# Weight chunks fetched and summed two chunks ahead of their split, and the third weight sum kept in the tile of the activation sums

## The chip, the cores and the metric

The kernel runs on one core of a Trainium2 chip. The metric is the time of one execution on the device in microseconds (us), as the median of several runs.

## The reference, cut to what matters

The kernel computes a two-layer trunk over 512 positions with 1024 features, in float32. The first layer mixes with a spatial gate and pooling heads, the second with a short gated convolution. Every layer then attends into a memory of 256 positions and runs a gated feed-forward block, and each of the three sub-layers ends in a layer norm of `alpha * x + f(x)`. The change touches only the way in which weights are fetched, and the down projection of the feed-forward block:

```python
def conv_ffn(x, w_up, conv_w, conv_b, w_down):
    up = x @ w_up
    a, g = up[..., :D_FF], up[..., D_FF:]
    g = causal_dwconv(g, conv_w) + conv_b
    return (jax.nn.gelu(g) * a) @ w_down        # 512 x 2816 @ 2816 x 1024
...
x = layer_norm(alpha * x + conv_ffn(x, ...), ln_ffn_g[layer], ln_ffn_b[layer])
```

## The kernel before, in words

**Products.** Every operand of a matrix product is split into a high and a low part: ScalarE copies the float32 value to a rounded one (`split`, L80), and VectorE subtracts that from the value to get the rest (L81). One product of two operands is then three matmuls into the same PSUM tile (`mm3`, L194 to L196): high by high, high by low, low by high.

**Weights.** All weights pass through `Weights` in the order of a list, `plan`. A chunk is 128 partitions by 1024 columns, 512 KB. It is fetched by a DMA that SyncE's queue issues into a raw tile (pool `rpool`, seven buffers), and split into a pair of tiles `wh` and `wl` (pool `wpool`, `RING` = 5 buffers each). When a chunk has been used, `done()` calls `load()`, which issues the fetch, the sums if there are any, and the split of the chunk five places ahead. Across engines nothing but data and free tiles orders the work: SyncE issues a transfer as soon as its raw tile is free, so it runs ahead of the splits. Each engine works off its own queue in order. That order is laid out when the program is built, from the order of the code and from when each instruction is expected to be ready. A tile goes to its next user when the last reader of its last user is done, and tiles of one pool are handed out in the order of the code.

**The feed-forward block.** Its 22 hidden tiles go in three groups (`FFN_GROUPS`): two of eight, and one of six. For each group the up projection runs first (`ffn_up`; two chunks for each hidden tile, a gate and a value), then the group's part of the down projection. The groups of eight use seven block products in place of eight (`fast_product`), four times in the whole kernel: two groups in each of two layers. The third group is multiplied in the plain way.

**Sums of activations.** In `ffn_up` a `Blocks` object takes the hidden tiles of a group in four pairs. For each pair VectorE writes four blocks into one float32 tile named `blocks` (2048 columns, pool `fpool`, one buffer), makes four sums in it (L238) and splits seven of the eight blocks in one go (1792 columns), into tiles of the pool `apool`.

**Sums of weights.** For the same scheme GpSimd makes sums of weight blocks in `fast()`. The chunks of one product are, in the order of `fast_plan`: four `b11b21` with a first sum (t1, L148; one `t1t1` chunk for two of them); four `t2b22` with three sums each, where t3 = b22 - b12 (L153), t2 = t3 + b11 (L154, written over b12) and t4 = b21 - t2 (L155); one `t4t4` chunk behind each two of these; and two `t3t3` chunks. The sums t1, t3 and t4 of two chunks share a raw tile of their own. t3 is made with its `t2b22` chunk and used last.

**The product.** `fast_product` has three phases. Phase 1 takes the `b11b21` and `t1t1` chunks: 24 groups of three matmuls, into six PSUM tiles (X, Z, Y, two each). It ends in six adds to the rows `x` (L328, VectorE). Phase 2 takes `t2b22` and `t4t4`: for each `t2b22` chunk two groups with its first half (L365), two with its half of t4 (L367) and two with its second half (L369), 24 groups in all. X and Y go on in the same PSUM tiles, which the adds have read; Z gets new ones. Phase 3 takes `t3t3`, eight groups.

Of the kernel before, what the change touches and what calls it, by code (L numbers as in the profile page):

```python
# [8 lines left out]
F32 = mybir.dt.float32  # L9
# [5 lines left out]
P = 128  # L15
# [10 lines left out]
CH = 1024  # L26
ALPHA = 4.0**0.25
EPS = 1e-5
WINDOWS = (2, 4, 8, 16)
RING = 5  # L30
FFN_GROUPS = ((0, 8), (8, 16), (16, 22))
PAD = 16

# [2 lines left out]
def kernel(ctx: ExitStack, tc: tile.TileContext, a: dict, out: bass.AP):  # L36
    nc = tc.nc
# [4 lines left out]
    apool = ctx.enter_context(tc.tile_pool(name="apool", bufs=12))  # L42
    wpool = ctx.enter_context(tc.tile_pool(name="wpool", bufs=RING))
    rpool = ctx.enter_context(tc.tile_pool(name="rpool", bufs=7))
    gpool = ctx.enter_context(tc.tile_pool(name="gpool", bufs=1))
    tpool = ctx.enter_context(tc.tile_pool(name="tpool", bufs=4))
    fpool = ctx.enter_context(tc.tile_pool(name="fpool", bufs=1))
# [5 lines left out]
    def nm(s):  # L53
        uid[0] += 1
        return f"{s}{uid[0]}"
# [7 lines left out]
    def slot(dtype=F32R):  # L63

        return apool.tile([P, 2 * CH], dtype, tag="act", name=nm("act"))

    def duo(tag="act"):
        if tag == "act":
            t = slot()
            return t[:, :CH], t[:, CH:]  # L70
        h = wpool.tile([P, CH], F32R, tag="wh", name=nm("wh"))
        l = wpool.tile([P, CH], F32R, tag="wl", name=nm("wl"))
        return h, l

    def raw_tile():
        return rpool.tile([P, CH], F32, tag="raw", name=nm("raw"))

    def split(h, l, src):

        nc.scalar.copy(h, src)  # L80
        nc.vector.tensor_sub(l, src, h.bitcast(F32))  # L81

    def load_split(src, tag):
        raw = raw_tile()
        nc.sync.dma_start(raw, src)
        h, l = duo(tag)
        split(h, l, raw)
        return h, l
# [14 lines left out]
    plan = []  # L103
    for layer in range(2):
# [10 lines left out]
        plan += [("xa_wo", layer, n, i) for n in range(2) for i in range(4)]  # L115
        for m0, m1 in FFN_GROUPS:
            plan += [("ffn_w_up", layer, i) for i in range(2 * m0, 2 * m1)]
# [5 lines left out]
    class Weights:  # L123


        def __init__(self):
            self.ready, self.loaded, self.taken = [], 0, 0
            self.kept = {}

        def fast(self, what, layer, i):  # L130

            w = a["ffn_w_down"][layer]
            half = [slice(0, 512), slice(512, CH)]

            def fetch(src):
                t = raw_tile()
                nc.sync.dma_start(t[:, : src.shape[-1]], src)
                return t

            def both(key):  # L140

                if i % 2 == 0:
                    self.kept[key] = raw_tile()
                return self.kept[key][:, half[i % 2]]

            if what == "b11b21":
                w0, w1 = fetch(w[0, i]), fetch(w[1, i][:, half[0]])
                nc.gpsimd.tensor_sub(both("t1"), w1[:, half[0]], w0[:, half[0]])  # L148
                return w0
            if what == "t2b22":  # L150
                w1, w0, t3 = fetch(w[1, i]), fetch(w[0, i]), both(("t3", i // 2))
                b12 = t2 = w1[:, half[0]]
                nc.gpsimd.tensor_sub(t3, w1[:, half[1]], b12)  # L153
                nc.gpsimd.tensor_add(t2, t3, w0[:, half[0]])  # L154
                nc.gpsimd.tensor_sub(both("t4"), w0[:, half[1]], t2)  # L155
                return w1
            return self.kept.pop({"t1t1": "t1", "t4t4": "t4", "t3t3": ("t3", i // 2)}[what])

        def load(self, parts=1, other=None):

            if self.loaded == len(plan):
                return
            key = plan[self.loaded]
            self.loaded += 1
            if key[0] not in a:
                w = duo("w")
                split(*w, self.fast(*key))
                self.ready.append(w)
                return
            src = a[key[0]][key[1:]] if key[1:] else a[key[0]]  # L170
            both = ([other] if other else []) + [(src, duo("w"))]
            raws = [raw_tile() for _ in both]
            n = src.shape[-1] // parts
            for p in range(parts):
                c = slice(p * n, (p + 1) * n)
                for raw, (source, (h, l)) in zip(raws, both):
                    nc.sync.dma_start(raw[:, c], source[:, c])
                    split(h[:, c], l[:, c], raw[:, c])
            self.ready.append(both[-1][1])

# [9 lines left out]
    weights = Weights()  # L190
# [31 lines left out]
    class Blocks:  # L222
# [8 lines left out]

        def new(self):

            f = fpool.tile([P, 8, 256], F32, tag="blocks", name=nm("blocks"))

            def finish():
                def sub(to, x, y, op=ALU.subtract):
                    nc.vector.tensor_tensor(f[:, to, :], f[:, x, :], f[:, y, :], op=op)  # L238

                sub(self.S1, self.A21, self.A22, ALU.add)  # L240
                sub(self.S2, self.S1, self.A11)
                sub(self.S3, self.A11, self.A21)
                sub(self.S4, self.A12, self.S2)
                h, l = (slot()[:, : 7 * 256].rearrange("p (b s) -> p b s", b=7) for _ in range(2))
                self.pairs.append((h, l))
                split(h, l, f[:, :7, :])

            return [f[:, self.A11 :: self.A21, :], f[:, self.A12 : self.A22 + 1, :]], finish
# [303 lines left out]
    def load_mem():  # L552
        return [load_split(a["memT"][i], "act") for i in range(2)]
# [110 lines left out]
    def ffn_up(layer, xT, late, m0, m1):  # L664
        fast = m1 < NF
        hid = Blocks() if fast else Act(m1 - m0)
        m = m0
        while m < m1:
            n = 2 if m == 0 else 1
            ps = proj_batch([("ffn_w_up", layer, m * 2 + i) for i in range(2 * n)], xT, late if m == 0 else None)  # L670
            for i in range(n):
                g = tmp()
                conv3(g, ps[2 * i], lambda j: convw[:, layer, m, j : j + 1], convb[:, layer, m : m + 1])
                nc.scalar.activation(g, g, AF.Gelu_apprx_tanh)  # L674
                if fast:
                    if m % 2 == 0:
                        to, finish = hid.new()
                    halves = [v.rearrange("p (i s) -> p i s", i=2) for v in (g, ps[2 * i + 1])]
                    nc.vector.tensor_mul(to[m % 2], *halves)  # L679
                    if m % 2:  # L680
                        finish()
                else:
                    nc.vector.tensor_mul(g, g, ps[2 * i + 1])
                    split(hid.h(m - m0), hid.l(m - m0), g)
                m += 1
        return hid


    xT = Act(KD)
    for k in range(4):  # L690
        weights.load(2 if k < 2 else 1, (a["xT"][k], xT.tiles[k]))
    weights.done(RING - 4)

    late = None
    mem = []
    for layer in range(2):
        if layer == 0:
            y = mixer_ab(xT)
            xT, late = residual_norm([(lambda: y, 0, 8)], "ab_w_out", "ln_mix", layer, ahead=lambda: mem.append(load_mem()))
            kT = proj_k(layer, mem[layer], {2: late})  # L700
            late = None
        else:
            kT = proj_k(layer, mem[layer], {2: late})
            y = mixer_c(xT)
            xT, late = residual_norm([(lambda: y, 0, 8)], "c_w_out", "ln_mix", layer)
        o, hooks = attend(layer, xT, late, kT)
        xT, late = residual_norm([(lambda: o, 0, 8)], "xa_wo", "ln_xa", layer, hooks=hooks)
        up = [(lambda m0=m0, m1=m1, xT=xT, late=late: ffn_up(layer, xT, late, m0, m1), m0, m1) for m0, m1 in FFN_GROUPS]
        xT, late = residual_norm(up, "ffn_w_down", "ln_ffn", layer, layer == 1,
                                 ahead=None if layer else lambda: mem.append(load_mem()))  # L710
# [57 lines left out]
def build(shapes):  # L768
    import concourse.bacc as bacc

    nc = bacc.Bacc("TRN2", target_bir_lowering=False, num_devices=1)
    aps = {n: nc.dram_tensor(f"in_{n}", s, F32, kind="ExternalInput").ap() for n, s in shapes.items()}
    out = nc.dram_tensor("out_0_dram", (1, S, D), F32, kind="ExternalOutput").ap()
    with tile.TileContext(nc) as tc:
        kernel(tc, aps, out)
    return nc
# [9 lines left out]
```

## Time and profile before

| | |
|---|---|
| median of 3 runs | 1373.07 us (1372.56 to 1373.35) |
| the profiled execution's own time | 1371.29 us |
| its span, from the first to the last instruction | 1369.5 us |
| TensorE (matmul) busy | 1335.1 us, 97% of the span |
| VectorE busy | 842.1 us, 61% |
| ScalarE busy | 498.1 us, 36% |
| GpSimd busy | 153.5 us, 11% |
| granted TensorE clock, mean | 0.989 |

The profiled execution's time is some 1.8 us above its span, which counts only from the first to the last instruction. In the profile PE is TensorE's matmuls, PEld its weight loads, DVE is VectorE, ACT ScalarE, POOL GpSimd, and SP SyncE (SPq: its queue, which issues DMAs). L81 is line 81 of the kernel. Tile names stand without their numbers, so every raw tile is `raw`. A granted clock of 1.00 is 2.4 GHz and 0.50 is 1.2 GHz; between them lies a stretch that has some of each.

### The profile page before, as it was taken

The numbers are of one execution on the slowest core, as the hardware profiler recorded it, in microseconds if no ns is written. First come the engines' busy times: TensorE is split into PE (matmuls) and PEld (weight loads), VectorE is DVE, ScalarE is ACT, GpSimd is POOL, SyncE is SP. The second block draws the span as 40 slices with busy tenths as digits, with TensorE's granted clock in tenths as the row PEclk, the third lists the DMA queues.
The fourth block names the chain that finished last, engine by engine and source line by source line (L and its number), as shares of the span: only waits on it lengthen the run. The fifth ranks groups of instructions, "written<-read, shape, count | busy, mean of one in ns | idle before, by whom it ended". The sixth has DMA issues, their size and how long they took to land.

```text
span 1369.5 us, 16418 instructions
## 1 busy us (share of the span) xinstructions
PE 1335.1 (97%) x6526; PEld 1130.9 (83%) x6526; DVE 842.1 (61%) x1102; ACT 498.1 (36%) x671; POOL 153.5 (11%) x132
## 2 busy tenths in 40 slices
PE   8999999999989998999999999999999989998996
PEld 6888888898868886888988888988898868886885
DVE  6668456576576656556744447565776675576446
ACT  5343345244333333342522222354243433342330
POOL 1102000011240123000100001000101420141001
PEclk9999999999999999999999999999999999999999
DMA  9533433133344234433523331542142253326201
GB/s 361 157 123 114 164 126 108 59 109 98 102 150 142 85 95 159 139 108 93 200 93 97 103 93 48 168 139 78 47 154 93 93 186 106 95 88 202 94 0 62
DMA packets 47454, 161.88 MB, mean 118 GB/s; under 512 B 5648, under 2 KB 5776, under 8 KB 47376
## 3 DMA queue, kind: packets, MB, share of 16 engines
q1 hardware_dynamic: 45648, 154.53, 35.0%
q0 software_dynamic: 1728, 6.29, 1.4%
q8 instruction: 51, 0.84, 0.2%
q14 instruction: 27, 0.22, 0.1%
HBM read 158.70 MB, written 2.10 MB: 117 GB/s over the span
## 4 chain that ended last, share of the span: by engine, by line
PE 90%; POOL 4%; DMA 3%; DVE 2%; issue 1%; ACT 1%; POOLq 0%; DVEq 0%
PE ps L194 29%; PE ps L195 29%; PE ps L196 29%; DMA raw<-in_ffn_w_down 3%; POOL raw L154 1%; PE ps L313 1%; POOL raw L153 1%; DVE wl L81 1%; POOL raw L155 1%; ACT wh L80 1%; PE ps L633 1%; POOL rs L285 0%; DVE x L288 0%; PE ps L510 0%; DMA raw<-in_xT 0%
## 5 line engine op out<-in xcount | busy, mean ns | idle before, releaser
L81 DVE TENSOR_TENSOR wl<-raw,wh 128x1024 fp32r<-128x1024 f32 (+1 forms) x275 | 357.1, 1301 | 314.8 <-ACT wh L80 302.2
L80 ACT CAST wh<-raw 128x1024 fp32r<-128x1024 f32 (+1 forms) x275 | 287.4, 1045 | 561.7 <-PE ps L195 264.9
L194 PE MATMUL ps<-act,wh 128*128 128x512 f32 (+1 forms) x1316 | 478.8, 364 | 0.0
L195 PE MATMUL ps<-act,wh 128*128 128x512 f32 (+1 forms) x1316 | 478.4, 363 | 0.0
L196 PE MATMUL ps<-act,wl 128*128 128x512 f32 (+1 forms) x1316 | 478.3, 363 | 0.0
L194 PE MATMUL ps<-wh,act 128*128 128x512 f32 (+1 forms) x678 | 268.9, 397 | 23.9 <-DVE x L328 19.2
L194 PEld LDWEIGHTS ps<-act,wh 128*128 128x128 f32 x1316 | 248.5, 189 | 39.0
L196 PEld LDWEIGHTS ps<-act,wl 128*128 128x128 f32 x1316 | 248.5, 189 | 38.8
L195 PEld LDWEIGHTS ps<-act,wh 128*128 128x128 f32 x1316 | 248.5, 189 | 38.5
L195 PE MATMUL ps<-wl,act 128*128 128x512 f32 (+1 forms) x678 | 266.7, 393 | 0.0
L196 PE MATMUL ps<-wh,act 128*128 128x512 f32 (+1 forms) x678 | 266.4, 393 | 0.0
L194 PEld LDWEIGHTS ps<-wh,act 128*128 128x128 f32 x678 | 130.0, 192 | 52.5 <-DVE x L328 20.9
L196 PEld LDWEIGHTS ps<-wh,act 128*128 128x128 f32 x678 | 129.6, 191 | 27.0
L195 PEld LDWEIGHTS ps<-wl,act 128*128 128x128 f32 x678 | 129.9, 192 | 26.3 <-DVE wl L81 0.4
L285 POOL TENSOR_TENSOR rs<-rs,mhalf 128x1 f32<-128x1 f32 x28 | 39.9, 1428 | 824.6 <-DVE rs L284 824.6
L80 ACT CAST act<-ps 128x256 fp32r<-128x256 f32 (+1 forms) x144 | 62.9, 470 | 120.5 <-PE ps L313 79.2
L81 DVE TENSOR_TENSOR act<-ps,act 128x256 fp32r<-128x256 f32 (+1 forms) x144 | 73.0, 535 | 13.5 <-ACT act L80 13.1
L537 DVE SCALAR_TENSOR_TENSOR tmp<-ps,convw,tmp 128x511 f32<-128x511 f32 x88 | 65.6, 746 | 1.5
L674 ACT ACTIVATE tmp<-tmp 128x512 f32<-128x512 f32 x44 | 27.9, 633 | 96.9 <-DVE tmp L537 96.8
L148 POOL TENSOR_TENSOR raw<-raw,raw 128x512 f32<-128x512 f32 x16 | 27.0, 1688 | 269.4 <-DVE wl L81 216.2
L679 DVE TENSOR_TENSOR blocks<-tmp,ps 128x512 f32<-128x512 f32 x32 | 22.0, 687 | 46.3 <-PE ps L196 40.3
L81 DVE TENSOR_TENSOR act<-blocks,act 128x1792 fp32r<-128x1792 f32 x16 | 33.6, 2098 | 23.7 <-ACT act L80 23.7
(75 smaller groups left out, 763.2 us busy)
## 6 DMA issues: line engine op xcount, KB each, us to landing
raw<-in_ffn_w_up SPq DMA_DIRECT2D x88, 512.0 KB, 3.6
raw<-in_ffn_w_down SPq DMA_DIRECT2D x60, 512.0 KB, 3.6
raw<-in_c_w_in SPq DMA_DIRECT2D x24, 512.0 KB, 3.6
raw<-in_xa_wk SPq DMA_DIRECT2D x16, 512.0 KB, 3.7
raw<-in_xa_wq SPq DMA_DIRECT2D x16, 512.0 KB, 3.8
raw<-in_xa_wv SPq DMA_DIRECT2D x16, 512.0 KB, 3.5
raw<-in_xa_wo SPq DMA_DIRECT2D x16, 512.0 KB, 4.0
raw<-in_ab_w_f SPq DMA_DIRECT2D x8, 512.0 KB, 7.7
```

Of the source, the lines that this page charges most:

```text
L80: nc.scalar.copy(h, src)
L81: nc.vector.tensor_sub(l, src, h.bitcast(F32))
L148: nc.gpsimd.tensor_sub(both("t1"), w1[:, half[0]], w0[:, half[0]])
L153: nc.gpsimd.tensor_sub(t3, w1[:, half[1]], b12)
L154: nc.gpsimd.tensor_add(t2, t3, w0[:, half[0]])
L194: nc.tensor.matmul(ps, lh, rh, start=start, stop=False, skip_group_check=more)
L195: nc.tensor.matmul(ps, lh, rl, start=False, stop=False, skip_group_check=more)
L196: nc.tensor.matmul(ps, ll, rh, start=False, stop=stop, skip_group_check=more)
L285: nc.gpsimd.tensor_tensor(rs, rs, mhalf, op=ALU.pow)
L537: nc.vector.scalar_tensor_tensor(dst[:, s:], src[:, : S - s], tap(2 - s), dst[:, s:], op0=ALU.mult, op1=ALU.add)
L674: nc.scalar.activation(g, g, AF.Gelu_apprx_tanh)
L679: nc.vector.tensor_mul(to[m % 2], *halves)
```

## The change

`load()` is cut in two. `fetch()` takes the next chunk of the plan, issues its DMAs and, for the chunks of a fast product, GpSimd's sums, and puts the float32 result in a list. `load()` fetches until three results are in the list, and splits the oldest: so fetches and sums stand two chunks (`AHEAD`) further ahead in the code than splits. The pairs of first chunks at the start of the kernel, with which the input is loaded, keep their way in `load_beside()`.

The third sum t3 no longer gets raw tiles. For the four `t2b22` chunks of a product one tile of the kind `blocks` is taken, 4 x 512 columns, from the pool of the activation sums, which still has one buffer; the `t3t3` chunks are read from it.

```diff
--- before.py
+++ after.py
@@ -28,6 +28,7 @@
 EPS = 1e-5
 WINDOWS = (2, 4, 8, 16)
 RING = 5
+AHEAD = 2
 FFN_GROUPS = ((0, 8), (8, 16), (16, 22))
 PAD = 16
 
@@ -74,6 +75,10 @@
 
     def raw_tile():
         return rpool.tile([P, CH], F32, tag="raw", name=nm("raw"))
+
+    def blocks_tile():
+
+        return fpool.tile([P, 2 * CH], F32, tag="blocks", name=nm("blocks"))
 
     def split(h, l, src):
 
@@ -123,8 +128,9 @@
     class Weights:
 
 
+
         def __init__(self):
-            self.ready, self.loaded, self.taken = [], 0, 0
+            self.ready, self.fetched, self.loaded, self.taken = [], [], 0, 0
             self.kept = {}
 
         def fast(self, what, layer, i):
@@ -148,33 +154,53 @@
                 nc.gpsimd.tensor_sub(both("t1"), w1[:, half[0]], w0[:, half[0]])
                 return w0
             if what == "t2b22":
-                w1, w0, t3 = fetch(w[1, i]), fetch(w[0, i]), both(("t3", i // 2))
+                w1, w0 = fetch(w[1, i]), fetch(w[0, i])
+                if i % 4 == 0:
+                    self.kept["t3"] = blocks_tile()
+                t3 = self.kept["t3"][:, (i % 4) * 512 : (i % 4 + 1) * 512]
                 b12 = t2 = w1[:, half[0]]
                 nc.gpsimd.tensor_sub(t3, w1[:, half[1]], b12)
                 nc.gpsimd.tensor_add(t2, t3, w0[:, half[0]])
                 nc.gpsimd.tensor_sub(both("t4"), w0[:, half[1]], t2)
                 return w1
-            return self.kept.pop({"t1t1": "t1", "t4t4": "t4", "t3t3": ("t3", i // 2)}[what])
-
-        def load(self, parts=1, other=None):
-
+            if what == "t3t3":
+                return self.kept["t3"][:, (i % 4) * 512 : (i % 4 + 2) * 512]
+            return self.kept.pop({"t1t1": "t1", "t4t4": "t4"}[what])
+
+        def fetch(self):
             if self.loaded == len(plan):
                 return
             key = plan[self.loaded]
             self.loaded += 1
             if key[0] not in a:
+                raw = self.fast(*key)
+            else:
+                src = a[key[0]][key[1:]] if key[1:] else a[key[0]]
+                raw = raw_tile()
+                nc.sync.dma_start(raw[:, : src.shape[-1]], src)
+                raw = raw[:, : src.shape[-1]]
+            self.fetched.append(raw)
+
+        def load(self):
+            while self.loaded < len(plan) and len(self.fetched) <= AHEAD:
+                self.fetch()
+            if self.fetched:
+                raw = self.fetched.pop(0)
                 w = duo("w")
-                split(*w, self.fast(*key))
+                split(*(t[:, : raw.shape[-1]] for t in w), raw)
                 self.ready.append(w)
-                return
-            src = a[key[0]][key[1:]] if key[1:] else a[key[0]]
-            both = ([other] if other else []) + [(src, duo("w"))]
+
+        def load_beside(self, parts, source, other):
+
+            key = plan[self.loaded]
+            self.loaded += 1
+            both = [(source, other), (a[key[0]][key[1:]], duo("w"))]
             raws = [raw_tile() for _ in both]
-            n = src.shape[-1] // parts
+            n = CH // parts
             for p in range(parts):
                 c = slice(p * n, (p + 1) * n)
-                for raw, (source, (h, l)) in zip(raws, both):
-                    nc.sync.dma_start(raw[:, c], source[:, c])
+                for raw, (src, (h, l)) in zip(raws, both):
+                    nc.sync.dma_start(raw[:, c], src[:, c])
                     split(h[:, c], l[:, c], raw[:, c])
             self.ready.append(both[-1][1])
 
@@ -231,7 +257,7 @@
 
         def new(self):
 
-            f = fpool.tile([P, 8, 256], F32, tag="blocks", name=nm("blocks"))
+            f = blocks_tile().rearrange("p (b s) -> p b s", b=8)
 
             def finish():
                 def sub(to, x, y, op=ALU.subtract):
@@ -688,7 +714,7 @@
 
     xT = Act(KD)
     for k in range(4):
-        weights.load(2 if k < 2 else 1, (a["xT"][k], xT.tiles[k]))
+        weights.load_beside(2 if k < 2 else 1, a["xT"][k], xT.tiles[k])
     weights.done(RING - 4)
 
     late = None
```

## Rows read from the trace of the kernel before

**Rows 1.** The page, part 1: busy us, share, instructions of each engine.

```profile
PE 1335.1 (97%) x6526; PEld 1130.9 (83%) x6526; DVE 842.1 (61%) x1102; ACT 498.1 (36%) x671; POOL 153.5 (11%) x132
```

**Rows 2.** Waits of PE: line, awaited; us in total, times, longest.

```profile
PE ps L194 <- DVE x L328: 19.2, 4, 4.9
PE ps L194 <- ACT wh L80: 4.7, 1, 4.7
```

**Rows 3.** The first fast product by stretches: length, busy us (count), clock, DMA.

```profile
core 0: us, PE busy (x) PEld busy (x) DVE busy (x) ACT busy (x) POOL busy (x), PEclk, DMA share, GB/s
375.50:391.80 16.30, 16.30 (x73) 13.49 (x72) 15.32 (x12) 7.96 (x7) 10.00 (x5) 1.00 0.25 73
...
395.40:400.10 4.70, 0.00 (x0) 0.00 (x0) 2.42 (x3) 1.04 (x1) 2.90 (x2) 0.79 0.14 28
400.10:406.90 6.80, 6.79 (x20) 5.40 (x21) 1.23 (x1) 1.87 (x2) 0.00 (x0) 0.65 0.78 284
```

**Rows 4.** The same view over all four fast products, its sum.

```profile
sum 181.00, PE 161.81 PEld 131.61 DVE 134.75 ACT 65.68 POOL 57.17; mean PE 40.45 PEld 32.90 DVE 33.69 ACT 16.42 POOL 14.29
```

**Rows 5.** The chain that ended last, 376 to 400.2: start, us, what.

```profile
389.87 3.60 DMA raw<-in_ffn_w_down
...
394.91 2.13 POOL raw L154
...
397.06 1.05 ACT wh L80
...
400.11 0.80 PE ps L194
```

**Rows 6.** Timeline of POOL: start, us, instruction, idle time before it.

```profile
362.15 1.29 POOL L153 TENSOR_TENSOR raw<-raw 128x512 f32<-128x512 f32 x1 [7.56 <-DVE wl L81]
...
367.32 1.28 POOL L155 TENSOR_TENSOR raw<-raw,raw 128x512 f32<-128x512 f32 x1 [2.50 <-DVE wl L81]
...
385.46 2.16 POOL L154 TENSOR_TENSOR raw<-raw,raw 128x512 f32<-128x512 f32 x1
387.69 2.15 POOL L155 TENSOR_TENSOR raw<-raw,raw 128x512 f32<-128x512 f32 x1
...
394.91 2.12 POOL L154 TENSOR_TENSOR raw<-raw,raw 128x512 f32<-128x512 f32 x1
```

**Rows 7.** Waits of SyncE's queue, 356 to 391.

```profile
SPq L137 <- POOL raw L155: 15.9, 3, 7.6
```

**Rows 8.** Timeline of DVE, 376 to 400.2.

```profile
376.50 0.91 DVE L238 TENSOR_TENSOR blocks<-blocks 128x256 f32<-128x256 f32 x1
377.33 2.31 DVE L81 TENSOR_TENSOR wl<-raw,wh 128x1024 fp32r<-128x1024 f32 x1
379.56 0.87 DVE L238 TENSOR_TENSOR blocks<-blocks 128x256 f32<-128x256 f32 x2
380.35 1.22 DVE L81 TENSOR_TENSOR wl<-raw,wh 128x1024 fp32r<-128x1024 f32 x1
382.20 2.03 DVE L81 TENSOR_TENSOR act<-blocks,act 128x1792 fp32r<-128x1792 f32 x1 [0.63 <-ACT act L80]
384.14 6.79 DVE L81 TENSOR_TENSOR wl<-raw,wh 128x1024 fp32r<-128x1024 f32 x3
390.86 3.06 DVE L328 SCALAR_TENSOR_TENSOR x<-x,ps 128x512 f32<-128x512 f32 x5
393.85 2.07 DVE L81 TENSOR_TENSOR wl<-raw,wh 128x1024 fp32r<-128x1024 f32 x1
398.14 1.31 DVE L81 TENSOR_TENSOR wl<-raw,wh 128x1024 fp32r<-128x1024 f32 x1 [2.23 <-ACT wh L80]
399.38 0.68 DVE L328 SCALAR_TENSOR_TENSOR x<-x,ps 128x512 f32<-128x512 f32 x1
```

**Rows 9.** Timeline of ACT.

```profile
378.48 1.06 ACT L80 CAST wh<-raw 128x1024 fp32r<-128x1024 f32 x1 [1.95 <-PE ps L196]
...
380.47 1.70 ACT L80 CAST act<-blocks 128x1792 fp32r<-128x1792 f32 x1 [0.93 <-DVE blocks L238]
```

## The prediction, on record before the changed kernel ran

> **What bounds the kernel now.** The first view to read is the page's busy times: TensorE is busy in 97% of the span [rows 1]. So only what makes TensorE stand still, or run slow, can move the time. The second view is the waits, kept to TensorE: apart from one wait of 4.7 us, all that is booked is four waits for the add of L328, 19.2 us in all [rows 2]. Those are one in each fast product, and there are four fast products. The third view puts numbers on one of them by stretches [rows 3]: phase 1 issues its 72 matmuls in 16.30 us, 0.2265 us each; TensorE goes on into phase 2 until 395.4, stands still for 4.70 us, and then has a granted clock of 0.65 over the next 6.80 us, a stretch partly at 1.2 GHz, before it is back at 2.4 GHz. A product has 168 matmuls of 512 columns (24 + 24 + 8 groups of three), so without a stall it would take 168 x 0.2265 = 38.1 us. The four take 181.0 us together [rows 4], 45.25 each. The loss is 7.2 us a product, 28.6 us in all: 4.7 of stillness and about 2.5 of half clock. 28.6 us (2.1%) is the most that a cure of this wait can give.
>
> The fourth view, the chain up to the restart at 400.11, says why [rows 5, 8]. The last add of phase 1 sits on VectorE behind the low-part subtraction (398.14) of the fourth `t2b22` chunk. That waited for ScalarE's copy (397.06), the copy for GpSimd's second sum (394.91), and that for a DMA (389.87) which could not go before GpSimd had finished the third chunk's sums. Below, c0 to c3 are the four `t2b22` chunks of a product. GpSimd's own rows [rows 6] show it starting c0's sums at 362.15, long before they are needed, and then standing idle in between: it waits for a raw tile to come free, then for data. SyncE's row shows the same starvation from its side, 15.9 us behind GpSimd's L155 [rows 7]. Seven raw tiles hold what was fetched, and the third sums take two of them from their making to the end of the product.
>
> **The change, part by part.** *The third sum in the tile `blocks`.* This frees two of seven raw tiles, so the transfers of c1 to c3 no longer go one after another between the sums; their 3.6 us apiece leave the chain. But that tile has one buffer, and until then it holds the activations' own sums: its last reader is the split of the last pair of blocks, the VectorE row of 1792 columns at 382.20, 2.03 long [rows 8]. The new t3 is the first of three sums (L153, then L154, then L155, each reading the one before), so no `t2b22` sum of a product can begin before that row ends. Where GpSimd now starts at 362.15, it would start at 384.2, and somewhat earlier still: with no sums running beside them, VectorE's subtractions at 376.50 (0.91) and the split at 377.33 (2.31) fall to the 0.43 (two in 0.87) and 1.22 of the rows without company. That makes the block sums ready at 378.9 instead of 380.4; ScalarE is then bound by its own copy before (378.48 + 1.06 = 379.54) [rows 9], so the copy of the blocks ends at 381.24 and VectorE's half at 383.3. I take 383.3 as the new start.
>
> *Twelve sums in one run.* With the data waiting, GpSimd goes from sum to sum. One takes 1.28 to 1.29 alone and 2.12 to 2.16 beside a split on VectorE [rows 6], plus 0.08 between two (385.46 + 2.16 to 387.69, where the next begins); the split grows alike, from 1.22 to 2.26 (three in 6.79) [rows 8]. What counts is the sixth sum (it completes t4 of c0 and c1) and the twelfth (t4 of c2 and c3). Bounds: six take 6 x 1.37 = 8.2 us alone, 6 x 2.23 = 13.4 always in company; twelve take 16.4 or 26.8. One split in company costs the sums about 0.95; c0's split falls in the first six, and three to four splits in all twelve, so I take 9.2 and 19.6, nearer to the lone rows because VectorE mostly waits here for the sums it would disturb. Sums done at 392.5 and 402.9.
>
> The adds on VectorE are a further company for which no row has a price: an add and a sum never run together before. By the row of a split beside a sum they would cost at most 6 x 0.61 x 0.4 = 1.4 us by the twelfth sum; nothing is the lower end, and I take nothing, since the add reads one operand from PSUM, where the split reads both from SBUF. The Trainium skill ("GPSIMD Engine Reference", section Specifications) states that GpSimd shares its SBUF interfaces with VectorE and meets contention from instructions that have two SBUF inputs; the splits' rows agree, and no run here shows the adds. By that rule the sum stays as it is; by the row of the split the second lateness below would be 2.6 instead of 1.2 us.
>
> *What is late next.* TensorE enters phase 2 at 391.8. Its order there is by the code: two groups with c0 (L365), then two with t4 (L367). Their second matmul needs the low part, at 391.8 + 1.36 + 0.23 = 393.4. t4 is there at 392.5 + 1.05 (ScalarE) + 2.3 (VectorE beside the next sums) = 395.9: a stall of 2.5 us (0.4 with everything at lone prices, 6.7 with everything in company). For the second pair TensorE comes to t4 fourteen groups into phase 2, 391.8 + 9.5 + 2.5 = 403.8, and t4 is ready at 402.9 + 1.05 + 1.22 = 405.2 with the sums over: 1.2 us more (0 to 3). c1, c2 and c3 themselves are ready before their turn by the same count. A product then takes 38.1 + 2.5 + 1.2 = 41.8, plus what the clock loses after two short stalls. The rows show only stalls of 4.7 us, which cost about 2.5 of half clock; between nothing and that I take half, 1.3. So 43.1 against 45.25: 2.15 less, 8.6 over four products.
>
> *Fetching two chunks ahead.* SyncE's queue is already ahead of the splits by as many transfers as raw tiles allow, and the seven tiles are the same. Outside the fast products a chunk has no sums, and no TensorE wait is booked there beyond one of 4.7 us [rows 2]. Raw tiles of the memory inputs queue behind two chunks more, 11 us at an up chunk's 24 matmuls x 0.2265 x 2, against the whole projection that runs before they are read: zero, hidden by those matmuls; if that cover were missing, it would be one transfer of 3.6 us, twice.
>
> Sum: the profiled execution took 1371.29 (span 1369.5 and 1.8 around it); 1371.29 - 8.6 = 1362.7. The median of the runs stands 1.78 above the profiled one: 1364.5.
>
> **The rivals.** *A, the order on VectorE stays as it is, and the kernel gets slower.* The six adds and the splits share one queue. In the rows before, five adds go, then c2's split, c3's split, and the sixth add last [rows 8], and TensorE's S4 product needs that sixth add (its PSUM tile is added to x before it goes on). If c3's split still stands ahead of it, the add waits for the eleventh sum, at 383.3 + 11/12 x 19.6 = 401.3, then 1.05 for the copy, 1.31 for the split, 0.61 for the add and 0.04 to the restart: 404.3 instead of 400.11, 4.2 a product, 16.8 in all: 1390. It decides from the point at which the eleventh sum ends after 397.03, where it ends now; even at lone prices it ends at 383.3 + 15.1 = 398.4. For it: the order of the rows. Against it: that order is laid out with when the sums are expected, and they now hang on the blocks' split. The sixth add may even fall behind more than this.
>
> *B, the add stands behind c2's split but ahead of c3's.* The eighth sum ends at 396.4; copy and split in company 3.3, the add 0.61: restart at 400.3, as now. No change, 1373.
>
> *C, the stall goes altogether.* At lone prices the first lateness is 0.4 and the second none; 27 to 28.6 us less: 1345. The rows of sums in company at just this place (385.46, 394.91, each over 2.1) speak against it.
>
> *D, the change doesn't do what it says:* the sums run ahead of the split in the code, but wait for the tile. This is part of the forecast, not beside it.
>
> **How the numbers follow.** Forecast 0.38 (its own range 1352 to 1371); A 0.27; B 0.20; C 0.08; something unforeseen 0.07, spread over all three signs. 0.2% is 2.7 us, about what a measurement of this kernel can tell from no change. Faster: 0.38 + 0.08 + 0.04 = 0.50; same 0.22; slower 0.28. The range leaves out C and the upper half of A: 1349 to 1391.
>
> **What would show it.** Right: GpSimd's first L153 of each product starts just behind VectorE's split of the blocks, its twelve sums follow without DMA waits, and TensorE has two short waits a product, for low parts of t4 (L81), in place of one for L328. Wrong: L153 starting near 362 (the tile is handed on earlier than I read it); a TensorE wait for L328 still ending the stall, at 404 or later (A) or at 400 (B); sums above 2 us throughout; a clock that still falls after the shorter stalls, or never does.

## The result and the profile after

The changed kernel takes 1357.71 us (median of 4 runs, 1357.55 to 1358.35), the kernel before took 1373.21 beside it (4 runs): a ratio of 0.9888 with a 95% interval of 0.9871 to 0.9905, so it is faster by 1.1%. The forecast was 1364.5, its own range 1352 to 1371.

First the span with its clock and the busy times. The span is 13.7 us shorter than before (1369.5), the busy times are almost those of [rows 1], and the mean granted clock rises from 0.989 to 0.998.

```profile
core 0: 1355.8 us, clock 0.998
...
PE 1329.4 (98%) x6526; PEld 1124.3 (83%) x6526; DVE 826.3 (61%) x1102; ACT 496.9 (37%) x671; POOL 151.1 (11%) x132
```

The waits of PE answer to [rows 2] (old L80/L81 is now L85/L86, L194 to L196 are L220 to L222, L328 is L354):

```profile
PE ps L221 <- DVE wl L86: 5.9, 4, 1.5
PE ps L220 <- DVE x L354: 5.7, 4, 1.4
PE ps L220 <- ACT wh L85: 4.6, 1, 4.6
```

In place of one wait of 4.7 to 4.9 in each fast product there are two of about 1.5: one for the low part of t4, as forecast, and one for the last add of phase 1, the place that rival B named. The four fast products by windows answer to [rows 3, 4]:

```profile
375.50:417.50 42.00, 39.02 (x170) 31.32 (x169) 29.77 (x32) 16.13 (x15) 19.16 (x12) 1.00 0.52 167
...
sum 168.10, PE 156.20 PEld 125.47 DVE 119.25 ACT 64.50 POOL 76.64; mean PE 39.05 PEld 31.37 DVE 29.81 ACT 16.12 POOL 19.16
```

168.1 against 181.0 is 12.9 of the 13.7 us of span. The third number from the end is the granted clock: 1.00 in each of the four products, where [rows 3] show 0.65 behind the stall.

GpSimd's timeline in the first product answers to [rows 6] (old L153 to L155 are L162 to L164):

```profile
383.27 1.29 POOL L162 TENSOR_TENSOR blocks<-raw 128x512 f32<-128x512 f32 x1 [28.70 <-DVE act L86]
...
387.26 2.28 POOL L162 TENSOR_TENSOR blocks<-raw 128x512 f32<-128x512 f32 x1
389.62 1.29 POOL L163 TENSOR_TENSOR raw<-blocks,raw 128x512 f32<-128x512 f32 x1
390.99 1.30 POOL L164 TENSOR_TENSOR raw<-raw,raw 128x512 f32<-128x512 f32 x1
...
400.40 1.29 POOL L163 TENSOR_TENSOR raw<-blocks,raw 128x512 f32<-128x512 f32 x1
401.77 1.29 POOL L164 TENSOR_TENSOR raw<-raw,raw 128x512 f32<-128x512 f32 x1
```

The first sum waits 28.70 us for VectorE's split of the blocks, which hands the tile over at 383.2. Then twelve sums run without an idle gap. The sixth ends at 390.99 + 1.30 = 392.29, the twelfth at 403.06. Note the eleventh, c3's second: it ends at 401.69. Before, the same sum ended at 397.03 [rows 6]. It comes 4.7 us later now, and yet TensorE waits less. VectorE's timeline, beside [rows 8], shows why:

```profile
381.16 2.03 DVE L86 TENSOR_TENSOR act<-blocks,act 128x1792 fp32r<-128x1792 f32 x1 [0.37 <-ACT act L85]
387.05 1.34 DVE L86 TENSOR_TENSOR wl<-raw,wh 128x1024 fp32r<-128x1024 f32 x1 [3.86 <-ACT wh L85]
388.62 2.73 DVE L354 SCALAR_TENSOR_TENSOR x<-x,ps 128x512 f32<-128x512 f32 x4 [0.24 <-PE ps L222]
392.03 3.55 DVE L86 TENSOR_TENSOR wl<-raw,wh 128x1024 fp32r<-128x1024 f32 x2 [0.68 <-ACT wh L85]
395.51 0.67 DVE L354 SCALAR_TENSOR_TENSOR x<-x,ps 128x512 f32<-128x512 f32 x1
397.85 1.34 DVE L86 TENSOR_TENSOR wl<-raw,wh 128x1024 fp32r<-128x1024 f32 x1 [1.67 <-ACT wh L85]
399.11 0.68 DVE L354 SCALAR_TENSOR_TENSOR x<-x,ps 128x512 f32<-128x512 f32 x1
402.80 2.60 DVE L86 TENSOR_TENSOR wl<-raw,wh 128x1024 fp32r<-128x1024 f32 x2 [3.01 <-ACT wh L85]
```

Before, the splits of c2 and of c3 both stood ahead of the sixth add. Now the sixth add (399.11) stands behind c2's split (397.85) and ahead of c3's (402.80). SyncE's queue, in the stretch of [rows 7], waits most for splits (old L137 is L143), and no longer for GpSimd's sums:

```profile
SPq L143 <- DVE wl L86: 24.9, 4, 10.5
```

Two theories of the gain follow. *The order:* the sums now hang on the split of the blocks, so the instruction order expects them late, and the adds are laid out ahead of late splits. *The raw tiles:* two more of the seven are free, so c3's transfers no longer stand between the sums, which is what the prediction argued.

### The profile page after: what moved, and what is told of

Read it like the earlier page. It is cut to its first block, busy times and chain, and to the rows that moved or that the text cites. A ratio compares the mean times of both kernels' runs of the same rounds, so it can differ in the third digit from the quotient of the medians.

```text
span 1355.8 us, 16402 instructions
## 1 busy us (share of the span) xinstructions
PE 1329.4 (98%) x6526; PEld 1124.3 (83%) x6526; DVE 826.3 (61%) x1102; ACT 496.9 (37%) x671; POOL 151.1 (11%) x132
## 4 chain that ended last, share of the span: by engine, by line
PE 83%; issue 8%; POOL 5%; DMA 2%; DVE 1%; ACT 1%; POOLq 0%; DVEq 0%; SPq 0%
PE ps L220 27%; PE ps L221 27%; PE ps L222 27%; DMA raw<-in_ffn_w_down 2%; POOL blocks L162 2%; POOL raw L163 1%; PE ps L339 1%; POOL raw L164 1%; ACT wh L85 1%; PE ps L659 1%; POOL raw L154 0%; DVE wl L86 0%; POOL rs L311 0%; DVE x L314 0%; PE ps L536 0%
## 5 line engine op out<-in xcount | busy, mean ns | idle before, releaser
L86 DVE TENSOR_TENSOR wl<-raw,wh 128x1024 fp32r<-128x1024 f32 (+1 forms) x267 | 332.2, 1244 | 319.1 <-ACT wh L85 310.9
L85 ACT CAST wh<-raw 128x1024 fp32r<-128x1024 f32 (+1 forms) x267 | 279.0, 1045 | 551.0 <-PE ps L221 265.4
L220 PE MATMUL ps<-act,wh 128*128 128x512 f32 (+1 forms) x1316 | 478.5, 364 | 0.0
L222 PE MATMUL ps<-act,wl 128*128 128x512 f32 (+1 forms) x1316 | 478.0, 363 | 0.0
L220 PEld LDWEIGHTS ps<-act,wh 128*128 128x128 f32 x1316 | 248.3, 189 | 38.8
L222 PEld LDWEIGHTS ps<-act,wl 128*128 128x128 f32 x1316 | 248.3, 189 | 38.7
L220 PE MATMUL ps<-wh,act 128*128 128x512 f32 (+1 forms) x678 | 264.3, 392 | 10.6 <-DVE x L354 5.7
L221 PE MATMUL ps<-wl,act 128*128 128x512 f32 (+1 forms) x678 | 263.9, 389 | 5.9 <-DVE wl L86 5.9
L222 PE MATMUL ps<-wh,act 128*128 128x512 f32 (+1 forms) x678 | 263.6, 389 | 0.0
L220 PEld LDWEIGHTS ps<-wh,act 128*128 128x128 f32 x678 | 127.6, 189 | 39.2 <-DVE x L354 7.3
L222 PEld LDWEIGHTS ps<-wh,act 128*128 128x128 f32 x678 | 127.7, 188 | 26.1
L85 ACT CAST act<-ps 128x256 fp32r<-128x256 f32 (+1 forms) x144 | 62.9, 470 | 120.3 <-PE ps L339 79.2
L86 DVE TENSOR_TENSOR act<-ps,act 128x256 fp32r<-128x256 f32 (+1 forms) x144 | 73.0, 535 | 13.4 <-ACT act L85 13.0
L86 DVE TENSOR_TENSOR act<-blocks,act 128x1792 fp32r<-128x1792 f32 x16 | 33.5, 2092 | 22.6 <-ACT act L85 22.6
```

Source lines behind the costliest of these rows:

```text
L220: nc.tensor.matmul(ps, lh, rh, start=start, stop=False, skip_group_check=more)
L221: nc.tensor.matmul(ps, lh, rl, start=False, stop=False, skip_group_check=more)
L222: nc.tensor.matmul(ps, ll, rh, start=False, stop=stop, skip_group_check=more)
```

## The experiments

Each ratio is to the kernel before, run on the same chip beside it, with its 95% interval. Line numbers shift a little from kernel to kernel; the tile names say which instruction is meant. One wait of 4.6 to 5.6 us for `wh`, at the start of the kernel, stands in every profile here, before and after; it has no part in the argument.

**The two parts, one at a time.** `ahead_only` has the lead of two chunks and t3 in raw tiles as before; `tile_only` is the changed kernel with the lead taken out.

```diff
# ahead_only
-                if i % 4 == 0:
-                    self.kept["t3"] = blocks_tile()
-                t3 = self.kept["t3"][:, (i % 4) * 512 : (i % 4 + 1) * 512]
+                t3 = both(("t3", i // 2))
# tile_only
-AHEAD = 2
+AHEAD = 0
```

> The other part alone: fetched and summed two chunks ahead, but t3 in raw tiles as before. Theory (the tile is all): the raw tiles starve as before, the stall for the sixth add is back with 4.7 us and a half clock: 1373, no change against the kernel before. Rival (the lead carries part of the gain): 1360 to 1370.

> The third sum lives in the tile of the activation sums, but nothing is fetched ahead of its split (AHEAD = 0). Theory: the gain comes from the raw tiles that t3 no longer takes; SyncE's queue runs ahead of the splits anyway, so the two chunks of lead are worth nothing: 1357.7, within 1.5 us of the changed kernel. Rival: the lead lets the sums go earlier and carries part of the gain: 1362 to 1373.

`ahead_only`: 1371.49, 0.9995 (0.9986 to 1.0004). `tile_only`: 1358.99, 0.9905 (0.9891 to 0.9918). The waits of PE, `ahead_only` first, then `tile_only`:

```profile
PE ps L216 <- DVE x L350: 18.9, 4, 4.8
```

```profile
PE ps L221 <- DVE wl L86: 5.9, 4, 1.5
...
PE ps L220 <- DVE x L354: 4.2, 3, 1.4
```

With the lead alone the old waits stay; with the tile alone they are nearly those of the changed kernel. The lead is worth nothing and the tile gives all of the gain.

**Is it the run of sums that sets the new end?** `t4_twice` makes every t4 sum twice over: sixteen sums a product in place of twelve.

```diff
-                nc.gpsimd.tensor_sub(both("t4"), w0[:, half[1]], t2)
+                t4 = both("t4")
+                for _ in range(2):
+                    nc.gpsimd.tensor_sub(t4, w0[:, half[1]], t2)
```

> GpSimd makes every t4 twice (the second time over the first, with the same values): 16 sums a product in place of 12. Theory: behind the split of the blocks the run of sums sets the time, so the last t4 comes 4 sums of 1.3 to 2.2 us later and the product 5 to 8.5 us, more if the clock falls again by 2.5: 1378 to 1402. Rival (the sums are hidden, and VectorE's queue or the data set the two waits that are left): 1357 to 1362.

1385.29, 1.0095 (1.008 to 1.0111): some 27 us more than the changed kernel, as the theory had it. The waits of PE, and the window behind the first stall:

```profile
PE ps L222 <- ACT wh L85: 27.7, 9, 4.8
PE ps L223 <- DVE wl L86: 3.5, 7, 0.5
```

```profile
396.00:400.20 4.20, 2.46 (x5) 1.55 (x6) 1.82 (x2) 1.17 (x2) 4.04 (x4) 0.55 0.63 209
```

TensorE now waits for copies, and the low parts behind them. So GpSimd's run has no slack left in the changed kernel, and the clock falls again (0.55) behind a stall of 3.5.

**The adds ahead of the last two loads.** In phase 1 the last two `done()`, which issue two later chunks, move behind the six adds. `adds_first` does this to the changed kernel, `before_adds_first` to the kernel before, with t3 in its raw tiles and no lead:

```diff
                 for p in halves:
                     mul(Y[p], Blocks.S1, i + j, p, part(t1, j), s, e)
-                weights.done()
-            weights.done()
+                if i + j < n - 1:
+                    weights.done()
+            if i < n - 2:
+                weights.done()
...
             add(p + 2, 1, Y[p])
+        weights.done(2)
```

> The changed kernel, but the six adds that end phase 1 stand ahead of the last two loads in the code, so that no split stands between the fifth and the sixth add on VectorE. TensorE's wait of 1.4 us for the sixth add goes. Theory (the twelfth sum sets the end): TensorE then comes 1.4 us earlier to the second t4, which is no earlier, and waits there instead: 1357.7, no change within 1.5 us. Rival (the order on VectorE costs what the wait shows): 4 x 1.4 less, 1352.

> The kernel before, t3 in raw tiles and no lead, with one edit: the six adds that end phase 1 stand ahead of the last two loads in the code, so that VectorE makes the sixth add before the splits of c2 and c3. Theory of the order (what TensorE waited for was an add behind a late split, not the late sums themselves): c3 is needed at 404, its sums end at 397, t4 of the first pair was ready at 390.9; the stall goes, and with it the half clock: 28 us less than before, 1344 to 1348, faster than the changed kernel. Theory of the raw tiles (the transfers between the sums are the cause): the sums stay as late as they are and TensorE still waits for them: 1365 to 1373.

`adds_first`: 1358.26, 0.9901 (0.9887 to 0.9914), no gain. The add's wait is gone, and 0.57 and 0.52 us of waiting now stand at the second t4, as rows of its PE timeline show:

```profile
405.95 0.73 PE L220 MATMUL ps<-wh,act 128*128 128x512 f32 x2 [0.57 <-ACT wh L85]
407.21 0.50 PE L221 MATMUL ps<-wl,act 128*128 128x512 f32 x1 [0.52 <-DVE wl L86]
```

`before_adds_first`: **1343.86**, 0.9787 (0.9774 to 0.98), 28.9 us faster than the kernel before, though nothing was done to the tiles. Its waits of PE, the window 391.8 to 400, and the timelines of GpSimd and VectorE:

```profile
PE ps L194 <- ACT wh L80: 4.7, 1, 4.7
```

```profile
391.80:400.00 8.20, 8.20 (x37) 6.61 (x36) 5.90 (x9) 2.66 (x4) 4.74 (x3) 1.00 0.54 191
```

```profile
393.86 1.29 POOL L153 TENSOR_TENSOR raw<-raw 128x512 f32<-128x512 f32 x1 [3.47 <-DMA raw<-in_ffn_w_down]
395.23 2.15 POOL L154 TENSOR_TENSOR raw<-raw,raw 128x512 f32<-128x512 f32 x1
```

```profile
391.39 3.66 DVE L328 SCALAR_TENSOR_TENSOR x<-x,ps 128x512 f32<-128x512 f32 x6
394.98 1.26 DVE L81 TENSOR_TENSOR wl<-raw,wh 128x1024 fp32r<-128x1024 f32 x1
```

GpSimd still idles 3.47 us for a transfer, and c3's second sum ends at 397.38, no earlier than in the kernel before. But all six adds run in one go, the stall of [rows 2] is gone, and TensorE runs 8.20 of 8.20 us at clock 1.00. So late sums alone do not stall TensorE; it took the add queued behind c3's split. The theory of the raw tiles is not enough to explain the stall. Whether earlier transfers, with the order left as it was, would have removed it too was not run.

**t3 half in raw tiles, half in the blocks' tile.** `t3_half_half` keeps t3 of c0 and c1 in a raw tile, so that sums may start early, and t3 of c2 and c3 in the other tile; `half_half_adds` has the edit on the adds too.

```diff
-                if i % 4 == 0:
-                    self.kept["t3"] = blocks_tile()
-                t3 = self.kept["t3"][:, (i % 4) * 512 : (i % 4 + 1) * 512]
+                if i % 2 == 0:
+                    self.kept["t3", i // 2] = blocks_tile() if i % 4 else raw_tile()
+                t3 = self.kept["t3", i // 2][:, half[i % 2]]
```

> The third sums of c0 and c1 go to a raw tile, those of c2 and c3 to the tile of the activation sums. Theory (the hand-over of that tile sets the start of the sums): the first pair's six sums run at 362 to 379 again and only six stay behind the split of the blocks, ending near 392.5; the wait for the first t4 goes, c3's split comes at 394 to 396.5, so the sixth add behind it costs 0 to 2 us: 1344 to 1352. Rival (one raw tile held is enough to starve the transfers): 1357 or more.

> The same with the six adds ahead of the last two loads in the code. Both theories of the cause taken together leave no wait in a product: 4 x 38.1 us against 181.0 before, 1344 to 1347. If a wait for a sum or for data is left, 1350 or more.

`t3_half_half` missed: 1375.45, 1.0019 (1.001 to 1.0028), where 1344 to 1352 was expected. Its waits of PE and timelines:

```profile
PE ps L220 <- DVE x L354: 21.0, 4, 6.0
```

```profile
395.17 1.27 POOL L162 TENSOR_TENSOR blocks<-raw 128x512 f32<-128x512 f32 x1 [3.87 <-DMA raw<-in_ffn_w_down]
396.52 1.26 POOL L163 TENSOR_TENSOR raw<-blocks,raw 128x512 f32<-128x512 f32 x1
```

```profile
398.88 1.32 DVE L86 TENSOR_TENSOR wl<-raw,wh 128x1024 fp32r<-128x1024 f32 x1 [4.62 <-ACT wh L85]
400.13 0.68 DVE L354 SCALAR_TENSOR_TENSOR x<-x,ps 128x512 f32<-128x512 f32 x1
```

With early sums the sixth add is back behind c3's split, c3's transfers still come late, and its second sum ends at 397.78 where it ended at 397.03. That is 0.75 us later, 3.0 over four products, and the kernel is 2.65 us slower. This is the mechanism of rival A, at a small size. `half_half_adds`, with the adds moved, takes **1342.69**, 0.9783 (0.977 to 0.9797), a little below the 1344 to 1347 expected and the lowest time here; its interval overlaps that of `before_adds_first`, so the tile adds nothing that could be told.

**Hold the sums in the kernel before.** `sums_held` ties the first `t2b22` sum of a product behind the split of the blocks, by a subtraction of one column that reads that split's low part. t3 stays in raw tiles, and there is no lead.

```diff
# Blocks, behind the split of the blocks
+                weights.gate = l[:, 0, :1].bitcast(F32)
# fast(), t2b22
+                if i % 4 == 0:
+                    nc.gpsimd.tensor_sub(t3[:, :1], self.gate, self.gate)
```

> The kernel before with one thing of the change alone: its first t2b22 sum of a product is tied behind the split of the last blocks (a subtraction of one column of that split's low part, by GpSimd, into a column that the sum then overwrites). t3 stays in raw tiles, no lead, the code of the adds is untouched. Theory of the order: what gained time was that the sums hang on the blocks' split, so that the adds are laid out ahead of c2's and c3's splits; and what still costs is the late start: 1356 to 1361, like the changed kernel. Theory of the raw tiles: with the tiles held as before and the sums later the stall grows: 1373 or more.

> The changed kernel unaltered, on the same chip as the others, for direct comparison: 1357 to 1359 by every theory.

1365.08, 0.9947 (0.9933 to 0.9961), between the two theories' numbers: holding the sums back, which should cost time, gains 7.7 us. VectorE's order has become that of the changed kernel, the sixth add (399.50) ahead of c3's split (404.67), as its timeline shows:

```profile
398.24 1.34 DVE L81 TENSOR_TENSOR wl<-raw,wh 128x1024 fp32r<-128x1024 f32 x1 [1.66 <-ACT wh L80]
399.50 0.67 DVE L331 SCALAR_TENSOR_TENSOR x<-x,ps 128x512 f32<-128x512 f32 x1
404.67 2.61 DVE L81 TENSOR_TENSOR wl<-raw,wh 128x1024 fp32r<-128x1024 f32 x2 [4.49 <-ACT wh L80]
```

`after_again`, the changed kernel once more beside it, takes 1358.03, 0.9893 (0.988 to 0.9907), another 7 us less. GpSimd's timeline in `sums_held`:

```profile
383.40 0.19 POOL L154 TENSOR_TENSOR raw<-act 128x1 f32<-128x1 f32 x1 [28.73 <-DVE act L81]
...
398.44 2.26 POOL L155 TENSOR_TENSOR raw<-raw 128x512 f32<-128x512 f32 x1
402.26 1.29 POOL L156 TENSOR_TENSOR raw<-raw,raw 128x512 f32<-128x512 f32 x1 [1.55 <-DMA raw<-in_ffn_w_down]
```

The 1.55 us of waiting for a transfer, in a run of sums with no slack, is where the two free raw tiles count once the sums start late: it is 1.36 to 1.72 us in the other three products, 6.1 us in all. The tie's own instruction puts the first sum 0.28 us later (383.68), 1.1 over four. Together they would make up the 7 us; the two were not separated.

**The sixth add tied behind c3's split, in the changed kernel.** This was to price rival A.

```diff
-        for p in halves:
-            add(p + 2, 1, Y[p])
+        add(2, 1, Y[0])
+        with tc.issue_after(weights.last.ins):
+            add(3, 1, Y[1])
```

> The changed kernel with the old order put back by hand: the sixth add is tied behind c3's split on VectorE. Theory of the order: the add comes after c3's split, which ends at 404.1 in the changed kernel, so TensorE's second wait grows from 1.4 to some 6 us and the product by 4.3 to 5, up to 2.5 more where the clock falls: 1375 to 1388, slower than before, although t3's tile and the lead are as in the changed kernel. Theory of the raw tiles: 1358 to 1363, since the sums are the same.

Another miss: 1359.33, 0.99 (0.9886 to 0.9914), where 1375 to 1388 was expected. VectorE's timeline and the waits of PE:

```profile
403.80 1.34 DVE L86 TENSOR_TENSOR wl<-raw,wh 128x1024 fp32r<-128x1024 f32 x1 [3.62 <-ACT wh L85]
405.06 0.68 DVE L354 SCALAR_TENSOR_TENSOR x<-x,ps 128x512 f32<-128x512 f32 x1
```

```profile
PE ps L220 <- ACT wh L85: 8.1, 3, 4.8
PE ps L221 <- DVE wl L86: 5.9, 4, 1.5
```

The add is about as late as A said, at 405.06, but no wait for it is booked: with the tie in place TensorE's order changed too, so that the group that needs this add must have moved behind others. What the tie would cost with TensorE's order kept was not shown.

**One raw tile fewer, adds moved.** `adds_first_raw6` is `before_adds_first` with `bufs=7` of `rpool` made 6.

> The kernel before with the six adds ahead of the last two loads, and six raw tiles in place of seven. Theory of the order: the sums have room (c3 is ready at 399.8 and needed at 406.6, the second t4 at 401.1 against 403.2), so that a raw tile less shows little: 1344 to 1350. Theory of the raw tiles: every tile counts, a stall of some us in each product comes back: 1356 or more.

1352.0, 0.9853 (0.9836 to 0.987), between the theories again: 8.1 us more than `before_adds_first`. TensorE waits for copies and low parts (9.1 us in 5 waits, one of them the 4.6 outside the products, and 3.0 in 4). Raw tiles have a price, but seven are enough once the adds are out of the way: no wait is booked in the products of `before_adds_first`.

## Why the prediction was right, and where it was not

**The hand-over of the tile** came as worked out: 383.2 against 383.3, and the first sum at 383.27. **The twelve sums** as well: the sixth ended at 392.29 (forecast 392.5), the twelfth at 403.06 (402.9). **t4's low part** of the first pair was ready at 392.03 + 3.55 = 395.58 (395.9). A product took 42.0 us, where the forecast had 41.8 before its term for the clock; of the 3.9 above the 38.1 of its matmuls, 2.9 are booked as waits, and the rest lies around them, some of it in matmuls that start further apart behind a wait (0.34 us below, against 0.2265). **The adds beside the sums** were priced at nothing, and so it is where the rows show it: the sum at 389.62 lies wholly beside the adds of 388.62 to 391.35 and took 1.29, while those that meet a split took 2.15 to 2.28. (The prediction's remark that an add and a sum never ran together before is not quite right: the five adds of [rows 8] end at 393.92, and a sum had begun at 393.54.) The Trainium skill ("GPSIMD Engine Reference", section Specifications) names instructions of VectorE with two SBUF inputs among those that contend with GpSimd. These rows agree.

**The mis-sized term is the clock.** 1.3 us a product was set aside for it, half of what a stall of 4.7 costs; in the profiled execution it cost nothing. That is 4 x 1.3 = 5.2 us, less 0.9 by which the four products took longer than 4 x 41.8: 4.3 of the 6.8 us between forecast and result. Another 1.65 is the gap between the profiled execution and the median, 1.78 in the forecast and 0.13 for the changed kernel (1357.58 and 1357.71), and 0.8 came off outside the products. The two waits were forecast at 2.5 + 1.2 and measured at 1.5 + 1.4. The first is smaller mostly because TensorE reached t4's low part later than worked out, at 394.16 against 393.4: ScalarE's copy of t4, which its first matmul needs, ended only at 393.37, and two matmuls with the copy stand ahead of the one with the low part. Its timeline shows both waits:

```profile
395.64 0.50 PE L221 MATMUL ps<-wl,act 128*128 128x512 f32 x1 [1.48 <-DVE wl L86]
395.98 0.40 PE L222 MATMUL ps<-wh,act 128*128 128x512 f32 x1
...
399.84 0.50 PE L220 MATMUL ps<-wh,act 128*128 128x512 f32 x1 [1.42 <-DVE x L354]
```

**The second wait stood elsewhere.** Not the second t4 ended it but the sixth add, behind c2's split: the order of rival B, and almost its time (restart at 399.84, forecast 400.3). B forecast no change from this, because it let TensorE come to that add at 395.4, as before. It came there at 398.42 now, 3.02 us later: 1.48 are the wait at t4, 0.91 are four more matmuls laid out ahead of the add (19 after 391.8 in place of 15, at 0.2265 each), and the rest is the wider spacing around that wait. So the time of the restart was right and the loss was not: a wait costs what is left of it when the engine arrives. With the add out of the way (`adds_first`) the second t4 came up in its place, for the same time in the end: the forecast's second lateness was there, and lay hidden under B's wait.

**The step that failed is the cause of the stall:** "the transfers of c1 to c3 no longer go one after another between the sums; their 3.6 us apiece leave the chain". The prediction took the late transfer, at the early end of the chain, for what held TensorE. Every link of that chain [rows 5] is there, and yet its early end alone does not stall TensorE: c3's second sum ends 4.7 us later in the changed kernel, and in `before_adds_first` it is no earlier than before while the stall is gone. The link that could be cut was the last one, an add whose data was there (in `before_adds_first` all six are done at 391.39 + 3.66 = 395.05, where the sixth began at 399.46 before), queued in order behind a subtraction that it did not need. The prediction named it ("sits on VectorE behind the low-part subtraction"), and A and B weighed its place, but no term of the forecast's own sum did. That the add left its place behind c3's split is what the sum took for granted; in this the forecast was partly lucky, and the gain came out at 15.5 us where 8.6 had been worked out.

So about half of the 15.5 us is a side effect. With the sums tied to the blocks' tile, one late split fewer stands ahead of the sixth add; `sums_held` gets 7.7 us with such a tie alone. (That the tie works by way of the times that are expected when the order is laid out is argued from how the order is made; the runs show only that the order changed.) The freed tiles then keep the late run of sums fed, which is most of another 7. With the adds moved, the change costs more than it gives: 1358.26 (`adds_first`) against 1343.86 (`before_adds_first`), 14.4 us, from two separate comparisons with the kernel before. The lead of two chunks does nothing either way. And the 28.6 us that the prediction called the most that a cure could give were all to be had by a few moved lines: 28.9 in `before_adds_first`.

Open: the price of rival A at its full size (`sixth_behind` moved TensorE's order as well), and what more raw tiles would do in the kernel before with t3 and the order left alone. Freeing one of the two, as `t3_half_half` does, was not enough: c3's first sum still waits 3.87 us for a transfer, and the stall stays.

## What to carry to other kernels

When the chain of waits ends in an instruction on an in-order engine, ask first whether that instruction's own operands were late or only the one queued ahead of it; here moving the ready add gave 28.9 us, and freeing tiles for the transfers behind its neighbour, with what else that moved, 15.5. An order laid out when the program is built can leave a ready instruction waiting for microseconds, and a change that shifts the order can then speed up a kernel in which the sums themselves got later: undo one part at a time before believing in the mechanism it was made for. And price a wait from when the waiting engine arrives, not from when its releaser is done.

## What the runs showed of the hardware that was not expected

The same program can keep its clock or lose it behind the same short wait. In the changed kernel's first profile the granted clock stayed at 1.00 in all four products, through a wait of 1.48 us in each. `after_again` is the same kernel in another execution: after a wait of 1.48 us for the same low part its matmuls start 0.43 us apart until 400.25, and the granted clock from 396.9 to 400.2 is 0.52, which is 1.2 GHz for nearly all of that stretch. It lost the clock in the first two products and kept it in the last two. Its rows of PE, the windows of its first and third product, and a wait of PE:

```profile
396.84 0.63 PE L221 MATMUL ps<-wl,act 128*128 128x512 f32 x1 [1.48 <-DVE wl L86]
397.27 0.63 PE L222 MATMUL ps<-wh,act 128*128 128x512 f32 x1
```

```profile
375.50:417.50 42.00, 40.44 (x171) 32.49 (x170) 28.62 (x31) 16.37 (x16) 19.18 (x12) 0.96 0.49 172
...
1076.70:1118.70 42.00, 39.02 (x170) 31.34 (x169) 28.65 (x31) 16.27 (x16) 19.17 (x12) 1.00 0.50 170
```

```profile
PE ps L220 <- DVE x L354: 2.8, 2, 1.4
```

`sixth_behind` does the same: 0.96 in its first two products and 1.00 in the last two, behind waits of 1.48 us each. So it is not the program alone that decides; what does was not tried.

In the changed kernel losing the clock cost nothing. From the wait in the first product to that in the second, `after_again` takes 128.94 us (396.84 to 525.78), the first profile 129.01 (395.64 to 524.65). Where the clock fell, TensorE came to the sixth add when it was already done: the wait for it is booked in two products in place of four.
